# A streaming encoder layer on one core: the last two weight pairs in two sets of tokens, other forms of both norms, and weight preparation moved

## The chip, the core and the metric

The kernel runs on one core of a Trainium2 chip. The metric is the device time of one launch in microseconds: three runs of the kernel before gave 2345.38, 2347.2 and 2352.4, median 2347.2. The engines are named as in the profile: PE (TensorE, PEld its weight loads), DVE (VectorE), ACT (ScalarE), POOL (GpSimd), SP (SyncE, whose queue issues all DMAs here).

## The reference

One layer over 2048 prompt tokens and 64 sample tokens, width 1024, with a gated feed-forward part of width 2816. All inputs are float32.

```python
def trunk_layer(x, ...):
    mix, new_conv, new_ssm, new_k, new_v = token_mixers(x, ...)   # SSD scan and windowed attention, w_in, w_out
    h = layer_norm(DEEPNORM_ALPHA * x + mix, ln1_g, ln1_b)
    y = layer_norm(DEEPNORM_ALPHA * h + swiglu(h, w_gate, w_up, w_down), ln2_g, ln2_b)
    return y, new_conv, new_ssm, new_k, new_v

def swiglu(h, w_gate, w_up, w_down):
    g = jnp.einsum('bld,df->blf', h, w_gate)
    u = jnp.einsum('bld,df->blf', h, w_up)
    return jnp.einsum('blf,fd->bld', jax.nn.silu(g) * u, w_down)
```

## The kernel before

Every float32 operand of a matmul is scaled and split into two float16 parts (high, low); `mm3` multiplies with three matmuls (lines 112 to 114). The prompt is cut into eight blocks of 256 tokens (two tiles `t` of 128 rows each); the sample tokens are block 8 (`NB`).

Three stages follow each other. The first runs the input projection and the mixers block by block, and writes `mix` to DRAM. The second, `out_proj` (lines 879 to 888), goes through the blocks tile by tile: `op_rows` multiplies with `w_out` (two psum halves, added to the residual at line 821), takes `layer_norm` (lines 789 to 797: statistics by `bn_stats`, root by `rsqrt`, lines 98 to 108, a bit trick and three Newton steps of three instructions each) and normalises on DVE (line 825). One tile later `op_cols` transposes the tile, scales the columns on ACT (line 843), writes the residual for the second part after two POOL instructions (line 847), and once both tiles of a block are there forms seven operands of a Strassen-like scheme (POOL differences, lines 870 to 875), each split by `put` (ACT line 854, DVE line 855). For blocks 0 to 3, five of the seven operands go directly into the tiles `B0`; the rest goes to DRAM (`hd`). Blocks 0 and 1 (`EARLY`) run beside the last mixers.

The third stage is the feed-forward part. The 2816 columns are 11 pairs (`NP_`) of 2 x 128. The tokens are processed in two halves, h = 0 (blocks 0 to 3) and h = 1 (blocks 4 to 7 and the sample). In each half a pair p runs `gate`, then `flush` (the down products of the pair before), then `up`. `products` (lines 1053 to 1083) makes seven products of 512 token columns in four psum banks; three of them (2, 4 and 3) resume a bank whose first content ACT has copied before. `prep_w(p, m)` loads, scales, combines and splits the weights in h = 0 and writes them to DRAM (`ws`); h = 1 loads them from there. `prep_d` does so for the down weights. `scheme(h, p)` says whether the down product uses the scheme, too: only in h = 1 for p < 9. After the last pair of a half `last` takes the second norm of a block: statistics (`row_stats` on ACT or `bn_stats` on DVE), one `rsqrt` for the two rows of a block, normalisation on ACT (line 1282), multiply and add of the norm's parameters (lines 1284 and 1285) on DVE and POOL, with exceptions in `EG`, and the write of the output. In h = 1 the last pair (`LAST`) runs `up` ahead of `flush`, which then makes the down products of pairs 9 and 10 together.

The instructions of each engine run in the order that the scheduler of the tile framework gave them from the program order, a priority (`tc.high_priority` moves the statistics forward) and its estimate of durations. The memory pools matter at one point: `p2` and `apool` (norm tiles, `w_out`) are closed after the last `op_cols`, and `p3r`, which holds the temporaries `a`, the down weights and the last two operand tiles, is opened in their place. The pool `p3` (weights `w0`, `w1`, `raw`) is open from the third block on.

## Time and profile before

| | us |
|---|---|
| median of three runs | 2347.2 |
| the profiled execution | 2346.7 |
| its span, first to last instruction | 2344.8 |
| PE busy | 2167.7 (92%) |
| DVE busy | 1841.0 (79%) |
| ACT busy | 997.3 (43%) |
| POOL busy | 602.0 (26%) |
| mean granted clock of PE | 0.971 |

Busy time of an engine counts an instruction from its start to its end, waits inside an instruction included. Idle time of PE, 177 us in all, lies in the first 100 us, in the second stage (700 to 1000), around the change of halves (1660 to 1720) and after the last matmul.

### The profile page before, as it was taken

To read this page: it belongs to the slowest core of one execution; us is meant where nothing else is said; L and a number is where in the kernel's file an instruction comes from. 1 tells how busy PE (TensorE), PEld (TensorE's weight loads), DVE (VectorE), ACT (ScalarE), POOL (GpSimd) and SP (SyncE) were. 2 spreads that over 40 slices of the span, in tenths; PEclk is the share of its full clock that TensorE was granted. 3 is DMA by queue.
4 is the path that set the end of the run, shared out by engine and by line. 5 is a ranking of instruction groups with operands and counts; after the bars stand their busy time and mean duration, and the time that the engine had idled before them with its cause. 6 is when DMAs were issued, how large, how long until landed. Compare 5 with 4: busy or idle time off the path is not lost. (4 is left out here: it accounts for less than half of the span.)

```text
span 2344.8 us, 37764 instructions
## 1 busy us (share of the span) xinstructions
PE 2167.7 (92%) x14422; PEld 1267.5 (54%) x14422; DVE 1841.0 (79%) x4227; ACT 997.3 (43%) x1966; POOL 602.0 (26%) x462
## 2 busy tenths in 40 slices
PE   6899999999979798699999999999899999999993
PEld 5677777877865344244444444444445455555551
DVE  7786787788778999768777777775978777777768
ACT  6354454454464443465444544542333333333223
POOL 2111111111123466623222312311422222222404
PEclk9899999999989999799999999999999999999997
DMA  7000100100232544564333433446442222222202
GB/s 220 26 22 24 33 24 19 37 33 11 70 108 63 188 160 162 179 230 149 117 127 124 157 103 125 150 153 220 162 152 88 89 91 91 90 91 90 68 5 76
DMA packets 136025, 241.97 MB, mean 103 GB/s; under 512 B 20768, under 2 KB 53796, under 8 KB 135844
## 3 DMA queue, kind: packets, MB, share of 16 engines
q1 hardware_dynamic: 135844, 239.56, 30.5%
q8 instruction: 113, 1.85, 0.3%
q14 instruction: 68, 0.56, 0.1%
HBM read 155.61 MB, written 83.91 MB: 102 GB/s over the span
## 5 line engine op out<-in xcount | busy, mean ns | idle before, releaser
L112 PE MATMUL ps<-B,w 128*128 128x512 f16 x1232 | 469.6, 382 | 27.1 <-ACT w L950 16.0
L114 PE MATMUL ps<-B,w 128*128 128x512 f16 x1232 | 466.8, 382 | 4.7 <-DVE w L951 4.7
L113 PE MATMUL ps<-B,w 128*128 128x512 f16 x1232 | 470.2, 382 | 0.0
L112 PEld LDWEIGHTS <-w 128*128 128x128 f16 x2808 | 273.4, 99 | 179.3 <-ACT w L950 16.9
L113 PEld LDWEIGHTS <-w 128*128 128x128 f16 x2808 | 272.7, 99 | 177.6 <-issue 26.1
L114 PEld LDWEIGHTS <-w 128*128 128x128 f16 x2808 | 273.8, 99 | 174.3 <-issue 8.5
L112 PE MATMUL mm<-x,w 128*128 128x256 f16 (+1 forms) x1224 | 315.2, 268 | 7.4 <-ACT cin L426 3.0
L114 PE MATMUL mm<-x,w 128*128 128x256 f16 (+1 forms) x1224 | 315.2, 268 | 1.3 <-DVE w L240 1.3
L113 PE MATMUL mm<-x,w 128*128 128x256 f16 (+1 forms) x1224 | 315.1, 268 | 0.0
L1176 DVE SCALAR_TENSOR_TENSOR acc<-pds,ai,acc 128x512 f32<-128x512 f32 x208 | 152.5, 743 | 37.1 <-PE pds L114 36.9
L1176 DVE SCALAR_TENSOR_TENSOR acc<-pd,ai,acc 128x512 f32<-128x512 f32 x216 | 153.8, 741 | 27.1 <-PE pd L114 25.4
L951 DVE SCALAR_TENSOR_TENSOR w<-raw,fsc,w 128x512 f16<-128x512 f32 x176 | 148.3, 882 | 29.5 <-ACT w L950 29.5
L112 PE MATMUL pds<-wd,act 128*128 128x512 f16 x384 | 145.5, 379 | 3.3 <-DVE acc L1176 3.3
L113 PE MATMUL pds<-wd,act 128*128 128x512 f16 x384 | 145.5, 379 | 0.0
L114 PE MATMUL pds<-wd,act 128*128 128x512 f16 x384 | 145.4, 379 | 0.0
L987 ACT ACTIVATE wd<-rawd,fsc 128x512 f16<-128x512 f32 x120 | 80.6, 715 | 145.0 <-DVE fsc L91 76.4
L1074 POOL TENSOR_TENSOR a<-a 128x512 f32<-128x512 f32 x44 | 57.0, 1295 | 315.1 <-ACT a L1073 296.3
L950 ACT ACTIVATE w<-raw,fsc 128x512 f16<-128x512 f32 x176 | 114.0, 711 | 53.7 <-POOL raw L959 25.8
L1127 ACT ACTIVATE act<-a,asc 128x512 f16<-128x512 f32 x111 | 72.1, 711 | 125.3 <-DVE asc L91 122.8
L112 PE MATMUL pso<-wo,mt 128*128 128x512 f16 (+1 forms) x272 | 104.2, 385 | 16.3 <-DVE x L821 13.2
L847 POOL TENSOR_TENSOR x<-x,gb 128x1024 f32<-128x1024 f32 (+1 forms) x34 | 83.1, 2443 | 94.1 <-PE pth L839 81.7
L113 PEld LDWEIGHTS <-act 128*128 128x128 f16 x636 | 62.1, 98 | 82.8 <-issue 13.3
(398 smaller groups left out, 4492.9 us busy)
## 6 DMA issues: line engine op xcount, KB each, us to landing
ws<-w SPq DMA_DIRECT2D x176, 256.0 KB, 2.3
w<-ws SPq DMA_DIRECT2D x176, 256.0 KB, 2.9
rawd<-in_w_down SPq DMA_DIRECT2D x22, 1024.0 KB, 6.5
x<-in_x_prompt SPq DMA_DIRECT2D x32, 512.0 KB, 3.9
raw<-in_w_gate SPq DMA_DIRECT2D x11, 1024.0 KB, 5.5
raw<-in_w_up SPq DMA_DIRECT2D x11, 1024.0 KB, 7.5
hd<-ht SPq DMA_DIRECT2D x41, 256.0 KB, 2.0
B<-hd SPq DMA_DIRECT2D x41, 256.0 KB, 6.0
```

What stands on the lines that cost most here:

```text
L112: T.matmul(out, lh, rh, start=start, stop=False, **kw)
L113: T.matmul(out, lh, rl, start=False, stop=False, **kw)
L114: T.matmul(out, ll, rh, start=False, stop=stop, **kw)
L847: G.tensor_tensor(out=r, in0=r, in1=gb1[:L, j], op=ALU.mult if j == 0 else ALU.add)
L950: S.activation(w[i][:, 0], x, AF.Identity, scale=sc)
L951: V.scalar_tensor_tensor(out=w[i][:, 1], in0=x, scalar=sc, in1=w[i][:, 0], op0=ALU.mult, op1=ALU.subtract)
L987: S.activation(w[i][:, 0], x, AF.Identity, scale=sc)
L1074: G.tensor_tensor(out=s["7"], in0=s["7"], in1=s["5"], op=ALU.add)
L1127: S.activation(at[:, 0], x, AF.Identity, scale=asc)
L1176: V.scalar_tensor_tensor(out=acc[:, cs], in0=ps, scalar=ai, in1=acc[:, cs], op0=ALU.mult, op1=ALU.add)
```

## The change

- A new `rsqrt1` finds the root of one column: the addition of epsilon is part of its first instruction, and a Newton step has two instructions in place of three. `layer_norm` uses it and returns the factor and the offset; `op_rows` normalises with them on ACT instead of DVE.
- `prep_w(0, 0)` and `prep_w(0, 1)` come after the output projection of blocks 2 to 5, ahead of blocks 6, 7 and the sample, instead of after all of them. `prep_d(0, 0)` stays where it was.
- In h = 1 the pairs 9 and 10 run in two sets, first blocks 4 and 5 with the sample, then blocks 6 and 7: gate and up of both pairs for a set, its down products, with the second set's gate and up laid between. `products` takes 256 columns of the operand tiles then, and the gate and up weights of both pairs are loaded a second time (`load_ws`).
- `last` takes the root row by row; in h = 1 it doesn't use POOL or ACT for the normalisation, but two DVE instructions that subtract, scale and shift. Both rows of block 6 have their statistics on ACT, both rows of block 7 on DVE. In h = 0 ACT, DVE and POOL keep their parts.

```diff
+    def rsqrt1(v, eps, y, L=P):
+        w = small.tile([P, 1], F32, tag="rsw1", name="rsw1")[:L]
+        V.tensor_scalar(out=v, in0=v, scalar1=eps, scalar2=0.5, op0=ALU.add, op1=ALU.mult)
+        V.tensor_scalar(out=y.bitcast(I32), in0=v.bitcast(I32), scalar1=1, scalar2=None,
+                        op0=ALU.arith_shift_right)
+        V.tensor_scalar(out=y.bitcast(I32), in0=y.bitcast(I32), scalar1=-1, scalar2=0x5EF759DF - 2 ** 31,
+                        op0=ALU.mult, op1=ALU.add)
+        for _ in range(3):
+            V.scalar_tensor_tensor(out=w, in0=y, scalar=v, in1=y, op0=ALU.mult, op1=ALU.mult)
+            V.scalar_tensor_tensor(out=y, in0=w, scalar=-1.5, in1=y, op0=ALU.add, op1=ALU.mult)
...
-        V.tensor_scalar(out=ag[:L, 1:2], in0=ag[:L, 1:2], scalar1=eps_, scalar2=None, op0=ALU.add)
-        V.tensor_copy(mu_r[:L, 0:1], ag[:L, 0:1])
-        rsqrt(ag[:L, 1:2], mu_r[:L, 1:2], 1, L, "rsw2")
+        rsqrt1(ag[:L, 1:2], eps_, mr[:L, 0:1], L)
+        V.scalar_tensor_tensor(out=mr[:L, 1:2], in0=ag[:L, 0:1], scalar=-1.0, in1=mr[:L, 0:1],
+                               op0=ALU.mult, op1=ALU.mult)
...
-        V.tensor_scalar(out=r, in0=r, scalar1=mr[:L, 0:1], scalar2=mr[:L, 1:2],
-                        op0=ALU.subtract, op1=ALU.mult)
+        S.activation(r, r, AF.Identity, scale=mr[:L, 0:1], bias=mr[:L, 1:2])
...
-    todo = out_proj([b for b in range(NB + 1) if b not in EARLY], psp, "p", todo)
-    op_cols(*todo[:3], psm, "mm")
...
+    HEAD = 4
+    rest = [b for b in range(NB + 1) if b not in EARLY]
+    todo = out_proj(rest[:HEAD], psp, "p", todo)
+    prep0()
+    todo = out_proj(rest[HEAD:], psp, "p", todo)
+    op_cols(*todo[:3], psm, "mm")
...
+    def load_ws(p, m, order):
+        wts[p, m] = w_tiles(p, m, order)
+        for i in order:
+            Q.dma_start(out=wts[p, m][i], in_=wsd[p][m][i])
...
-                mm3(ps, w[i][:, 0, k], w[i][:, 1, k], B[i][:, :, 0, k], B[i][:, :, 1, k],
+                mm3(ps, w[i][:, 0, k], w[i][:, 1, k], B[i][:, g.qs, 0, k], B[i][:, g.qs, 1, k],
...
-                if end and j == 0 and b != 7:
+                if end and (b == 6 or j == 0 and b != 7):
...
-            rsqrt(v, rs, n, L)
+            for j in range(n):
+                rsqrt1(mv[:, j, 1:2], LN_EPS / ALPHA ** 2, rs[:, j:j + 1], L)
...
+            if end:
+                V.scalar_tensor_tensor(out=r, in0=r, scalar=mv[:, j, 0:1], in1=gb[2][:L, 0],
+                                       op0=ALU.subtract, op1=ALU.mult)
+                V.scalar_tensor_tensor(out=r, in0=r, scalar=rs[:, j:j + 1], in1=gb[2][:L, 1],
+                                       op0=ALU.mult, op1=ALU.add)
...
+    p, p1 = NP_ - 2, NP_ - 1
+    ga, gs, gb_ = Group(Bt, blocks(4, 6)), groups[1], Group(Bt, blocks(6, 8))
+    gate(p, [ga, gs])
+    flush(pend)
+    get_w(1, p1, 0)
+    get_w(1, p, 2)
+    up(1, p, [ga, gs])
+    get_w(1, p1, 1)
+    gate(p1, [ga, gs])
+    load_ws(p, 0, ORD)
+    get_w(1, p1, 2)
+    up(1, p1, [ga, gs])
+    load_ws(p, 1, ORD)
+    gate(p, [gb_])
+    norms2()
+    for g in (gs, ga):
+        for rows in g.rows:
+            prod(p, g, rows)
+            prod(p1, g, rows)
+    load_ws(p1, 0, ORD)
+    up(1, p, [gb_])
+    load_ws(p1, 1, ORD)
+    for g in (gs, ga):
+        for rows in g.rows:
+            last(rows, True)
+    gate(p1, [gb_])
+    up(1, p1, [gb_])
+    for rows in gb_.rows:
+        prod(p, gb_, rows)
+    for rows in gb_.rows:
+        prod(p1, gb_, rows)
+        last(rows, True)
```

## Rows read from the trace of the kernel before

**Rows 1.** The page: span, and busy us (share) xinstructions of each engine

```profile
span 2344.8 us, 37764 instructions
PE 2167.7 (92%) x14422; PEld 1267.5 (54%) x14422; DVE 1841.0 (79%) x4227; ACT 997.3 (43%) x1966; POOL 602.0 (26%) x462
```

**Rows 2.** Busy time by stretch: PE, PEld, DVE, ACT, POOL, granted clock, DMA share

```profile
876.01:902.00 25.99, 23.20 (x114) 11.17 (x113) 25.16 (x46) 10.05 (x25) 15.47 (x9) 1.00 0.58 192
...
960.00:980.00 20.00, 5.52 (x19) 2.32 (x20) 9.11 (x15) 4.07 (x12) 18.40 (x9) 0.59 0.48 170
980.00:1020.00 40.00, 36.18 (x149) 15.66 (x148) 23.30 (x39) 22.35 (x38) 9.02 (x7) 0.88 0.92 334
1640.00:1720.00 80.00, 67.58 (x422) 32.13 (x420) 78.32 (x152) 24.92 (x35) 32.89 (x16) 0.96 0.53 173
...
2280.00:2300.00 20.00, 20.00 (x139) 10.20 (x136) 18.06 (x60) 6.95 (x13) 0.00 (x0) 1.00 0.00 1
...
2305.50:2344.80 39.30, 0.03 (x1) 0.00 (x0) 32.71 (x55) 7.01 (x6) 20.93 (x8) 0.57 0.30 113
```

**Rows 3.** Timelines of DVE and POOL, second stage (start, us, engine, line, operation)

```profile
850.93 1.19 DVE L107 SCALAR_TENSOR_TENSOR rsw<-rsw,ag 128x1 f32<-128x1 f32 x1
...
876.89 1.19 DVE L107 SCALAR_TENSOR_TENSOR rsw<-rsw,ag 128x1 f32<-128x1 f32 x1
878.11 2.27 DVE L108 SCALAR_TENSOR_TENSOR mr<-rsw,mr 128x1 f32<-128x1 f32 x1
...
881.84 0.16 DVE L108 SCALAR_TENSOR_TENSOR mr<-rsw,mr 128x1 f32<-128x1 f32 x1
882.03 0.16 DVE L106 TENSOR_TENSOR rsw<-mr 128x1 f32<-128x1 f32 x1
...
886.90 5.44 DVE L855 TENSOR_TENSOR ht<-hs,ht 128x512 f16<-128x512 f32 x2
...
886.68 5.10 POOL L847 TENSOR_TENSOR x<-x,gb 128x1024 f32<-128x1024 f32 x2
```

**Rows 4.** Groups of instructions by shape: count, busy us, mean ns, idle before, releasers

```profile
L951 DVE SCALAR_TENSOR_TENSOR w<-raw,fsc,w 128x512 f16<-128x512 f32 x176 | 148.3, 882 | 29.5 <-ACT w L950 29.5
...
L825 DVE TENSOR_SCALAR x<-x,mr 128x1024 f32<-128x1024 f32 x16 | 15.6, 977 | 0.2
...
L1282 ACT ACTIVATE acc<-acc,nb,rs 128x1024 f32<-128x1024 f32 x16 | 18.9, 1231 | 52.8 <-DVE nb L1279 38.9 <-DVE rsw L107 13.9
```

**Rows 5.** Timelines of DVE, PE and ACT around the first gate

```profile
951.51 0.72 DVE L821 SCALAR_TENSOR_TENSOR x<-pso,iv,x 64x512 f32<-64x512 f32 x1
...
979.84 0.61 PE L112 MATMUL ps<-B,w 128*128 128x512 f16 x1 [13.64 <-ACT w L950]
...
988.00 0.60 ACT L1065 ACTIVATE a<-ps 128x512 f32<-128x512 f32 x1 [2.18 <-DMA hds<-ht]
```

**Rows 6.** PE's timeline, 256-column matmuls; then one 512-column piece of the chain

```profile
285.08 0.27 PE L114 MATMUL mm<-x,w 128*128 128x256 f16 x1
285.19 0.27 PE L112 MATMUL mm<-x,w 128*128 128x256 f16 x1
...
2291.50 0.22 PE pds L113
```

**Rows 7.** Timelines of DVE and POOL after the last matmul

```profile
2305.00 9.09 DVE L1277 TENSOR_SCALAR mv<-mv 128x2 f32<-128x2 f32 x1
...
2338.59 2.36 DVE L1285 TENSOR_TENSOR acc<-acc,gb 128x1024 f32<-128x1024 f32 x2
...
2304.85 4.63 POOL L1284 TENSOR_TENSOR acc<-acc,gb 128x1024 f32<-128x1024 f32 x2
```

**Rows 8.** DVE's timeline: five 512-column additions, one 128-column product; statistics by shape

```profile
1714.43 3.37 DVE L1176 SCALAR_TENSOR_TENSOR acc<-pd,ai,acc 128x512 f32<-128x512 f32 x5
...
2261.03 0.34 DVE L1108 SCALAR_TENSOR_TENSOR sgs<-pss,invs,sgs 128x128 f32<-128x128 f32 x1
...
L1274 DVE BATCH_NORM_STATS2 bs<-acc 128x6 f32<-128x512 f32 x26 | 17.7, 683 | 0.2
```

More of the change, by code (lines that the diff above doesn't have):

```diff
@@ L966, in prep_w, with prep0 @@
         wts[p, m] = w
+    def prep0():
+        for m in range(2):
+            prep_w(0, m)
+    HEAD = 4
[4 more added lines that the diff above has]
+    op_cols(*todo[:3], psm, "mm")
+    es_2.close()
+    es_w.close()
+    p3r = pool("p3r", ctx, bufs=1, side="right")
     def prep_d(h, p):
@@ L1019, in get_w @@
         else:
-            wts[p, m] = w_tiles(p, m, ORD + (0,))
-            for i in ORD + (0,):
-                Q.dma_start(out=wts[p, m][i], in_=wsd[p][m][i])
+            load_ws(p, m, ORD + (0,))
     sB = p3.tile([P, 2, 2, 4, DSEQ], F16, name="sB")
@@ L1051, in products_sample, with products @@
         return ps
-    def products(w, B):
-        s = {}
+    def products(w, g):
+        s, B = {}, g.B
+        tile4 = lambda x: x.rearrange("p (b c) -> p b c", b=4)[:, :g.nq]
         for i in ORD:
@@ L1094, in gate @@
                 continue
-            s = products(wts[p, 0], g.B)
+            s = products(wts[p, 0], g)
             g.sg = {}
@@ L1111, in up @@
             else:
-                s = products(wts[p, 1], g.B)
+                s = products(wts[p, 1], g)
                 for j, c in enumerate(CS):
@@ L1130, in put @@
             def put(i, x):
-                act[i] = (p3.tile([P, 2, 4, P], F16, tag="w0", bufs=10, name="actl") if (h, p) == LAST else
-                          p3r.tile([P, 2, 4, P], F16, tag="act", bufs=7, name="act"))
+                if g.nq == 4:
+                    act[i] = p3r.tile([P, 2, 4, P], F16, tag="act", bufs=7, name="act")
+                else:
+                    if i % 2:
+                        two[0] = p3r.tile([P, 2, 2, 2, P], F16, tag="act", bufs=7, name="act2")
+                    act[i] = two[0][:, (i - 1) % 2]
                 split(act[i], x)
+            two = [None]
             if g.sub:
@@ L1251, in row_stats @@
         junk = p3r.tile([P, 2, 512], F16, tag="wd", bufs=9, name="junk").rearrange("p l d -> p (l d)")[:L]
-        sm = small.tile([P, 2], F32, tag="sm", bufs=2, name="sm")
+        sm = small.tile([P, 2], F32, tag="sm", bufs=6, name="sm")
         S.activation(junk, r, AF.Identity, accum_out=sm[:L, 0:1])
@@ L1262, in last @@
         L = P if b < NB else DSEQ
-        mv = small.tile([P, 2, 2], F32, tag="mv", bufs=2, name="mv")[:L]
-        rs = small.tile([P, 2], F32, tag="mr", name="rs2")[:L, :n]
+        mv = small.tile([P, 2, 2], F32, tag="mv", bufs=6, name="mv")[:L]
+        rs = small.tile([P, 2], F32, tag="rs2", bufs=6, name="rs2")[:L, :n]
         nb = small.tile([P, 2], F32, tag="nb", name="nb")[:L, :n]
@@ L1288, in last, with prod, flush @@
                              O["y_s"].rearrange("b l d -> (b l) d")), in_=r)
-    LEAD = 1
     PRI = 400
-    EG = {(4, 0): (G, G), (4, 1): (G, G), (6, 1): (V, V), (7, 0): (G, V), (7, 1): (V, V)}
-    def flush(*pends):
-        if not pends[0]:
-            return
-        h, p, groups = pends[0]
-        end = pends[-1][1] == NP_ - 1
-        if end:
-            norms2()
-        steps = [(g, rows) for g in reversed(groups) for rows in g.rows]
-        def prod(q, g, rows):
-            if rows is g.rows[0]:
-                ai = g.acts[q][1]
-                V.tensor_tensor(out=ai, in0=ai, in1=invs[:, q, 2:3], op=ALU.mult)
-            if g.sub:
-                down_sample(q, g)
-                return
-            if q == 0:
-                for row in rows:
-                    acc_init(*row)
-            if scheme(h, q):
-                down(q, g, rows[0][0])
-                return
-            for row in rows:
-                down_rows(q, g, row, len(pends) == 2)
-        ahead = LEAD if len(pends) == 2 else 0
-        for i in range(len(steps) + ahead):
-            if i < len(steps):
-                prod(p, *steps[i])
-            if i >= ahead:
-                if len(pends) == 2:
-                    prod(pends[1][1], *steps[i - ahead])
-                if end:
-                    last(steps[i - ahead][1], h == 1)
-    for m in range(3):
-        get_w(0, 0, m)
+    def prod(q, g, rows):
+        if rows is g.rows[0]:
+            ai = g.acts[q][1]
+            V.tensor_tensor(out=ai, in0=ai, in1=invs[:, q, 2:3], op=ALU.mult)
+        if g.sub:
+            down_sample(q, g)
+            return
+        if q == 0:
+            for row in rows:
+                acc_init(*row)
+        if scheme(g.h, q):
+            down(q, g, rows[0][0])
+            return
+        for row in rows:
+            down_rows(q, g, row, g.nq < 4)
+    def flush(pend):
+        if not pend:
+            return
+        p, groups = pend
+        if p == NP_ - 1:
+            norms2()
+        for g in reversed(groups):
+            for rows in g.rows:
+                prod(p, g, rows)
+                if p == NP_ - 1:
+                    last(rows, False)
+    get_w(0, 0, 2)
     pend = None
+    blocks = lambda b0, b1: [[(b, 0), (b, 1)] for b in range(b0, b1)]
     for h in range(2):
```

60 lines of the change are left out of this document (25 added, 35 removed).

## The prediction, made before the change was run

> **What bounds the kernel now.** I read the page first: TensorE is busy for 92% of a span of 2344.8 us [rows 1], so some 177 us of idle TensorE is all that an edit of order can win; the work on TensorE itself stays the same. Next I read the busy time by stretch, to find where those 177 us lie. Three stretches matter here.
>
> First, the output projection with its norms (about 700 to 955). In a stretch of one block TensorE is busy for 23.2 of 26.0 us, VectorE for 25.2 [rows 2]. The timeline of VectorE shows the same block returning after 25.96 us, with no room in it [rows 3]. A good part of it isn't work: the tiny steps of the root (128x1) take 0.16 us when alone and 1.19 or 2.27 us while GpSimd runs, and two 512-column differences take 5.44 us beside a 5.10 us GpSimd pair [rows 3]. The trace thus shows VectorE instructions with two inputs in SBUF waiting until the GpSimd instruction ends. I count about 10 us of such waits in a block, 16 us of work.
>
> Second, the hole before the first gate: in 960 to 980 TensorE is busy for 5.5 of 20 us at a granted clock of 0.59 (between the levels of 1.2 and 2.4 GHz), and the next 40 us have 0.88 [rows 2]. The second product of pair 0 stops 13.64 us for ScalarE's weight instruction (L950), and the first copy of a product comes only at 988.00, released by the last write of the sample block [rows 5]. So the weights of pair 0 come late, and, apart from that, so does the memory that the old stage holds (p3r takes the place of p2 and apool).
>
> Third, the end: TensorE ends at about 2305.5, and 39.3 us follow with VectorE at 32.7 and GpSimd at 20.9 us [rows 2]. A 128x2 addition takes 9.09 us there, next to GpSimd's 4.63 us pairs [rows 7].
>
> Before that end, from 1720, TensorE is full (20.00 in 2280 to 2300 [rows 2]).
>
> **First norm.** Per tile of 128 rows VectorE loses the separate add, the copy, three of nine root steps and the 128x1024 normalisation, and gains one small product. In steps of 0.19 us for the dependent ones (881.84 to 882.03 [rows 3]) that is 3 x 0.19 + 0.07 + 0.1 - 0.19 = 0.55 us, plus the normalisation, at 0.98 us mean [rows 4], its 0.75 us step when unblocked: 1.3 us a tile, 2.6 a block. ScalarE gets 1.23 us instead [rows 4]; it has about 10 us busy in 26 [rows 2], so it hides there, and the tile is used one tile later, so its latency hides too. TensorE's own 23.2 us [rows 2] are the new floor, so a block falls from 25.96 to about 23.7: 2.2 us. From 803 to 950 there are 5.7 blocks: 12.5 us; the two blocks mixed with the last mixers before that I put at 4. Gain 16 (bounds 5, if the waits for GpSimd just shift, and 20).
>
> **Pair 0's weights amid the projections.** This moves two prep_w with all they issue: per matrix eight ScalarE puts, as many VectorE puts (0.88 mean), four GpSimd sums [rows 4], the absolute maxima, one maximum on TensorE, and the writes to ws on SP's queue, which now stand before the loads of the last blocks (their loads run one to two tiles early, so I put that at nothing; cover gone, it would be one landing, some 4 us). Unblocked, VectorE's part is 16 x 0.67 + 1.5 = 12 us, and GpSimd's 8 sums (half as wide as the pair of rows 3, so some 1.3 us each) bring waits: at the block's ratio (10 us of waits to 15 of GpSimd) 7 us. VectorE is full there, so the stage grows by 19 us (bounds 12 and, with every put blocked for a GpSimd pair as in rows 3, 32).
>
> What it buys: the sample block's second half is added at 951.51, and the first copy follows 36.5 us later [rows 5]. Without the preparation between them there stays the sample's own chain (root 2, normalisation 1.2, transposes 1, columns 3, splits and two writes) beside what GpSimd has left of block 7 and the sample, eight instructions of 1.3 to 2.5 us (14.5), and the last write (2): some 17 us. So 19.5 us return (bounds 14 and 25). What is late next is the memory of p3r and the load of the two last operand tiles, not the weights. After it, the down weights of pair 0 can be fetched earlier, since their buffer is free earlier, and the clock falls less: of 3.8 us idle and about 4 us of clock in 980 to 1020 [rows 2] I take 4 back.
>
> Front: 16 - 19 + 19.5 + 4 = 20.5 us gained, I take 20; bounds 0 and 42 (the hole closes wholly and TensorE bounds all).
>
> **Norms between the halves (h = 0).** They keep the ScalarE normalisation and GpSimd, but take the root row by row: 2 x 10 small instructions in place of 13 a block, 7 more, four blocks. VectorE is full there (78.3 of 80 in 1640 to 1720 [rows 2]). 28 x 0.1 to 0.19 us is 3 to 5 us, some hidden by TensorE's work. I take a loss of 3 (bounds -2 and +8).
>
> **Last two pairs in two sets.** Gate and up run on 256 columns, twice: 672 matmuls in place of 336. A 256-column matmul of the projections starts 0.11 us after the one before, with a load of its own each; one of 512 takes 0.22 [rows 6]. So TensorE's time stays within 1 us. Here a rule speaks against it: the Trainium skill, TensorE: Matmul & The Clock Gate, The mechanism, says that a weight load overlaps a running matmul only if their row groups differ; all of these loads use all rows. The 0.11 us spacing of rows 6 speaks against such a charge; I give it a rival below. The new loads of ws (28 of 256 KB) go on SP's queue behind buffers that the previous gate or up frees, 10 us or more ahead of use; the share of DMA in 2280 to 2300 is 0.00 [rows 2], so I put them at nothing; without cover one load is some 3 us.
>
> VectorE gets more. A 128-column instruction takes 0.34, one of 512 0.67 in a row of five [rows 8]; so 256 costs about 0.4 and a split pair 0.13 more: 40 pairs, 5 us. The norms' two products of 1024 move to it: nine more at 1.18 [rows 7], 10.6 us. From the gate of the second set to the last matmul TensorE has 9 + 25 + 27 + 21 = 82 us; VectorE's work from there to the end is (leftover up 7.5, gates 3, ups 14, adds of the down products 24 x 0.67 + 2.6, five norms of the first set 22, the last four rows 21) = 86 us. It fits, though with little slack.
>
> The new end: in the last 5.2 us of TensorE and after, VectorE has 4 additions (2.6), two rows with statistics on ScalarE (0.45 + 9 x 0.15 + 2 x 1.18 = 4.1 each) and two with its own (2 x 0.6 [rows 8] + 0.15 + 1.35 + 2.36 = 5.1 each): 21 us, so it ends about 16.5 us after TensorE with a us of chain, and the last write takes what it takes now, 3.9 us (2344.8 less 2340.95 [rows 1, 7]). 20.4 in place of 39.3: 19 us gained if VectorE has no backlog. For waits of TensorE in the half-width sets and some backlog I take off 5: 14 (bounds 3 and 20).
>
> **Sum.** The profiled run took 2346.7 us, its span 2344.8 and 1.9 around it; the median of the three runs is 2347.2, so the sum stands half a us below what I compare with. 2346.7 - 20 + 3 - 14 = 2315.7, say 2316.
>
> **Rivals.**
> A: the front gives nothing. The weights' preparation lengthens the full VectorE stretch by the 32 us of its upper bound, which cancels the hole's 19.5 + 4 and half of the first norm's gain. For it: VectorE's waits [rows 3]. Against: ScalarE's share relieves it. 2346.7 + 3 - 14 = 2336.
> B: the end gains little. VectorE's 86 us run 11 us behind, so that the last rows' norms queue behind the first set's. For: 86 of 98 us available. Against: no GpSimd lock there any more. 2346.7 - 20 + 3 - 3 = 2327.
> C, slower: TensorE waits for ScalarE within the half products. Products 2, 4 and 3 resume a bank that ScalarE must have copied, and the cover falls from one product of 12 x 0.22 = 2.6 us to 1.3. There are 8 such calls, 24 points. A copy takes about 0.4 us, so it costs only if something stands before it, a row statistic for instance. At 1.2 us each it is 29 us, which leaves the kernel as it was; from 1.6 us each (38 us) it is slower, about 2355. Against: ScalarE is busy for 7 of 20 us in 2280 to 2300 [rows 2].
> D, slower too: the weight load isn't covered at half width. 336 more loads, each taken as long as the half matmul that follows it (0.11), are 37 us: 2353. That the projections keep a spacing of 0.11 with a load for each [rows 6] speaks against. The skill's rule above would give this one.
> E: the hole closes and TensorE bounds the whole front (42), the end gives 17: 2346.7 - 42 - 17 = 2288, with the half norms at nothing. For: TensorE needs just 23.2 us a block. Against: the memory of p3r still comes after the sample's chain. If the change doesn't do what it says, because the preparation is still put behind the last blocks on the engines' queues, the front is 12.5 + 4: 2346.7 - 16 + 3 - 14 = 2320, inside the forecast's range.
>
> **Chances.** Forecast 0.62 (that last case within it), A 0.14, B 0.10, E 0.08, C 0.04, D 0.02. A measurement of this kernel can tell about 0.3%, 7 us, from no change: faster is below 2340. Faster: 0.60 of the forecast, 0.10 of A, 0.10 of B and 0.08 of E: 0.88. Within: 0.02 of the forecast and 0.04 of A: 0.06; slower: C and D, 0.06. The range: forecast's sum with half of each bound gives 2300 to 2334; it must reach A's 2336 and towards E's 2288: 2293 to 2337 leaves about 0.2 out (most of E, C and D, and the forecast's and A's far ends).
>
> **What would show it.** In the profile after: L951 of pair 0 before the last blocks' additions; TensorE's idle 955 to 980 cut to under 10 us; a block period under 24.5 us; the normalisation of x on ScalarE with 1.2 us; GpSimd idle after the last pair; TensorE full in the half sets at a spacing of 0.11; about 20 to 24 us from its last matmul to the end. It would be wrong if VectorE's full stretch grows by more than 25 us, if the hole stays, or if TensorE shows idle time between the half products.

## The result, and the profile after

| | before | changed |
|---|---|---|
| timed, us: median (range, runs) | 2349.8 (2345.4 to 2353.0, 4) | 2320.7 (2320.1 to 2322.4, 4) |
| ratio, 95% interval | | 0.9875 (0.9856 to 0.9895) |
| profiled execution, span, us | 2344.8 | 2320.6 |

2316 was predicted, with 2293 to 2337 around it: the time lies in the range, 4.7 us above the forecast. The spans of the two profiled executions are only 24.2 us apart, the medians 29.1. Of the 4.9 us between these two figures 3.6 lie ahead of the change: the first addition of the output projection (VectorE, block 0) starts here, before, then changed.

```profile
712.52 0.75 DVE L821 SCALAR_TENSOR_TENSOR x<-pso,iv,x 128x512 f32<-128x512 f32 x1 [0.39 <-PE pso L114]
716.09 0.75 DVE L833 SCALAR_TENSOR_TENSOR x<-pso,iv,x 128x512 f32<-128x512 f32 x1 [0.52 <-PE pso L126]
```

Up to this addition every kernel of this document runs 1829 VectorE instructions, and no edit touches one of them; still its start varies from 710.4 to 716.1 us between the profiled executions. Counted from it, kernels with the same front reach the first copy of a product within 0.2 us of each other (266.3 to 266.5 in four of them). So where times of two executions are compared, they are counted from the first addition. The span counted so is 1632.3 us before and 1604.5 changed: 27.8 us apart, near the 29.1 of the medians.

The page of the changed kernel, against [rows 1]: span and busy us of each engine.

```profile
span 2320.6 us, 38579 instructions
PE 2172.3 (94%) x14762; PEld 1302.8 (56%) x14762; DVE 1834.2 (79%) x4264; ACT 1015.0 (44%) x2006; POOL 579.5 (25%) x457
```

TensorE's work has hardly changed (2172 for 2168 us); the gain is idle time. Busy time by stretch in the changed kernel, against [rows 2]; columns as there: PE, PEld, DVE, ACT, POOL, granted clock, DMA share, GB/s.

```profile
850.00:902.00 52.00, 49.04 (x245) 24.20 (x244) 50.86 (x87) 28.42 (x55) 36.28 (x20) 1.00 0.57 194
902.00:928.00 26.00, 19.37 (x82) 8.49 (x81) 24.53 (x29) 12.60 (x25) 21.35 (x13) 0.87 0.64 220
...
960.00:980.00 20.00, 16.02 (x76) 7.91 (x75) 18.12 (x23) 11.63 (x28) 15.89 (x8) 0.93 0.41 154
980.00:1020.00 40.00, 36.81 (x165) 16.73 (x165) 22.55 (x46) 21.25 (x36) 8.36 (x6) 0.92 0.80 284
...
1640.00:1720.00 80.00, 68.72 (x416) 32.17 (x414) 79.25 (x167) 27.87 (x41) 30.34 (x16) 0.94 0.52 179
...
2280.00:2300.00 20.00, 19.56 (x99) 9.38 (x98) 15.34 (x34) 3.40 (x7) 0.00 (x0) 1.00 0.00 0
2301.40:2320.60 19.20, 0.04 (x1) 0.00 (x0) 15.05 (x54) 1.58 (x4) 0.00 (x0) 0.57 0.28 109
```

Three things stand here. The hole of 960 to 980 is mostly filled (16.0 for 5.5 us of TensorE), but a new dent has come at 902 to 928, where the first pair's weights are now prepared: TensorE 19.4 of 26 us at a granted clock of 0.87 (between the levels of 1.2 and 2.4 GHz). And behind the last matmul 19.2 us are left where there were 39.3, without GpSimd.

Timelines of the changed kernel around the first gate, first VectorE, then TensorE, then ScalarE, against [rows 5] (start, us, engine, line, operation, idle before and its releaser).

```profile
964.60 0.73 DVE L833 SCALAR_TENSOR_TENSOR x<-pso,iv,x 64x512 f32<-64x512 f32 x1
...
983.19 0.59 PE L124 MATMUL ps<-B,w 128*128 128x512 f16 x1 [6.70 <-ACT a L1082]
...
970.93 1.24 ACT L837 ACTIVATE x<-x,mr 64x1024 f32<-64x1024 f32 x1 [4.46 <-DVE mr L809]
...
982.54 0.60 ACT L1082 ACTIVATE a<-ps 128x512 f32<-128x512 f32 x1 [1.68 <-DMA hds<-ht]
```

L833 is the second-half addition of the sample (L821 before), L1082 the first copy of a product (L1065 before). From the one to the other it is 17.9 us, where it was 36.5; but the addition comes 13.1 us later (964.60 for 951.51), 9.5 counted from the first addition. So the hole closed as forecast, and the first copy is only 9.0 us earlier (266.5 for 275.5, counted).

### The profile page after: what moved, and what is told of

It reads as the page before. It is cut to its first block, busy times and chain, and to the rows that moved or that the text cites. A ratio compares the mean times of both kernels' runs of the same rounds, so it can differ in the third digit from the quotient of the medians.

```text
span 2320.6 us, 38579 instructions
## 1 busy us (share of the span) xinstructions
PE 2172.3 (94%) x14762; PEld 1302.8 (56%) x14762; DVE 1834.2 (79%) x4264; ACT 1015.0 (44%) x2006; POOL 579.5 (25%) x457
## 5 line engine op out<-in xcount | busy, mean ns | idle before, releaser
L124 PE MATMUL ps<-B,w 128*128 128x512 f16 (+1 forms) x1344 | 486.0, 363 | 10.3 <-ACT a L1082 6.7
L125 PE MATMUL ps<-B,w 128*128 128x512 f16 (+1 forms) x1344 | 487.0, 363 | 0.0
L126 PE MATMUL ps<-B,w 128*128 128x512 f16 (+1 forms) x1344 | 484.0, 362 | 0.0
L125 PEld LDWEIGHTS <-w 128*128 128x128 f16 x2920 | 283.8, 99 | 167.3 <-issue 24.5
L126 PEld LDWEIGHTS <-w 128*128 128x128 f16 x2920 | 285.0, 99 | 156.7 <-issue 7.1
L124 PEld LDWEIGHTS <-w 128*128 128x128 f16 x2920 | 284.9, 99 | 153.3 <-issue 6.7
L956 DVE SCALAR_TENSOR_TENSOR w<-raw,fsc,w 128x512 f16<-128x512 f32 x176 | 151.3, 898 | 33.1 <-ACT w L955 33.1
L1199 DVE SCALAR_TENSOR_TENSOR acc<-pd,ai,acc 128x512 f32<-128x512 f32 x216 | 153.2, 742 | 21.6 <-PE pd L126 20.1
L124 PE MATMUL pds<-wd,act 128*128 128x512 f16 x416 | 158.1, 380 | 7.9 <-DVE acc L1199 7.4
L125 PE MATMUL pds<-wd,act 128*128 128x512 f16 x416 | 158.2, 380 | 0.0
L126 PE MATMUL pds<-wd,act 128*128 128x512 f16 x416 | 157.3, 380 | 0.0
L1091 POOL TENSOR_TENSOR a<-a 128x512 f32<-128x512 f32 (+1 forms) x48 | 59.0, 1228 | 365.9 <-ACT a L1090 326.6
L1144 ACT ACTIVATE act<-a,asc 128x512 f16<-128x512 f32 (+1 forms) x123 | 76.4, 683 | 128.2 <-DVE asc L91 125.5
L125 PEld LDWEIGHTS <-act 128*128 128x128 f16 x668 | 65.6, 98 | 86.3 <-issue 14.0
L126 PEld LDWEIGHTS <-act 128*128 128x128 f16 x668 | 65.2, 98 | 81.6 <-DVE act L1145 3.5
## 6 DMA issues: line engine op xcount, KB each, us to landing
w<-ws SPq DMA_DIRECT2D x204, 256.0 KB, 3.0
ws<-w SPq DMA_DIRECT2D x176, 256.0 KB, 2.1
hd<-ht SPq DMA_DIRECT2D x41, 256.0 KB, 2.0
B<-hd SPq DMA_DIRECT2D x41, 256.0 KB, 5.4
```

What stands on the lines that cost most here:

```text
L124: T.matmul(out, lh, rh, start=start, stop=False, **kw)
L125: T.matmul(out, lh, rl, start=False, stop=False, **kw)
L126: T.matmul(out, ll, rh, start=False, stop=stop, **kw)
L956: V.scalar_tensor_tensor(out=w[i][:, 1], in0=x, scalar=sc, in1=w[i][:, 0], op0=ALU.mult, op1=ALU.subtract)
L1091: G.tensor_tensor(out=s["7"], in0=s["7"], in1=s["5"], op=ALU.add)
L1144: S.activation(at[:, 0], x, AF.Identity, scale=asc)
```

## The experiments

Two tables carry the argument. A marker is an instruction that both kernels have: the sample's second-half addition, the first copy, and an up-projection of the second half (the first product of a pair with its gate, L1132 in the changed kernel, at 2037.5 before). In the second half the up-projections follow one another every 59.2 us in all kernels, so the last marker is the cleanest; in the first half the up-projection can stand before or behind a few products of the pair before. All times in us; those of the first table count from the first addition, whose own start stands in the third column. Counted so, the kernel before has 239.0, 275.5, 1325.0 and 1632.3.

**The front, with the new end in all four:**

| kernel | timed median | first addition | sample's addition | first copy | marker | end of span |
|---|---|---|---|---|---|---|
| neither edit at the front | 2333.8 | 713.3 | 238.9 | 275.3 | 1323.8 | 1616.7 |
| first norm alone | 2322.5 | 714.1 | 226.6 | 260.8 | 1314.2 | 1607.1 |
| moved preparation alone | 2338.4 | 715.7 | 256.0 | 276.4 | 1327.5 | 1620.4 |
| both (the changed kernel) | 2320.7 | 716.1 | 248.5 | 266.5 | 1311.3 | 1604.5 |

**The end, with the new front in all four:**

| kernel | timed median | marker (start in the span) | last matmul ends | marker to there | from there to the end |
|---|---|---|---|---|---|
| old order, old norms | 2335.2 | 2025.7 | 2293.8 | 268.0 | 39.6 |
| old order, new finish | 2327.1 | 2026.7 | 2294.8 | 268.0 | 29.9 |
| two sets, old finish | 2332.7 | 2025.9 | 2308.0 | 282.1 | 21.5 |
| two sets, new finish (changed) | 2320.7 | 2027.4 | 2301.4 | 274.1 | 19.2 |

"Finish" is what follows the root: normalisation, product and sum. The second and third rows both have the short root, which the first hasn't, so it is counted with either edit.

**The preparation put back.** The rest is the changed kernel.

```diff
-    todo = out_proj(rest[:HEAD], psp, "p", todo)
-    prep0()
-    todo = out_proj(rest[HEAD:], psp, "p", todo)
+    todo = out_proj(rest, psp, "p", todo)
...
+    prep0()
     get_w(0, 0, 2)
```

> The changed kernel, with the first pair's preparation put back behind all blocks; the short root, the ACT normalisation and the new end stay. Theory from the forecast (the move costs 19 us among the projections, returns 19.5 us of the hole and 4 us of clock): this kernel is 4.5 us slower than the changed one, some 2325 us. Rival from the changed kernel's trace (the sample's second-half addition came 13.1 us later although the norms had gained about 9.6, so the move costs 22.7; the hole shrank from 36.5 to 17.9, so it returns 18.6): the move is worth nothing, this kernel lies within 4 us of the changed one on the other side, 2317 to 2321 us. In its trace the sample's second-half addition should stand near 942 us and the first copy of a product some 36 us later, near 978.

2322.5 us (2321.7 to 2323.7), 1.8 above the changed kernel: between the two theories, and too little to tell from nothing. The addition stands at 940.7 and the first copy at 975.0, as expected. So with the new norm, counted from the first addition, the move costs 21.9 us of the projections (226.6 to 248.5) and takes 16.3 out of the hole (34.2 to 17.9). Another 8.8 us come back between the first copy and the up-projection at 1585.4 (869.3 counted, for 872.5 without the move). In all the move gains 2.9 us at the marker. Part of the 8.8 is visible as TensorE's idle time from 1100 to 1580, 7.3 us without and 3.8 with the move; the rest isn't traced to an instruction.

**The old first norm.**

```diff
-        rsqrt1(ag[:L, 1:2], eps_, mr[:L, 0:1], L)
-        V.scalar_tensor_tensor(out=mr[:L, 1:2], in0=ag[:L, 0:1], scalar=-1.0, in1=mr[:L, 0:1], ...)
+        V.tensor_scalar(out=ag[:L, 1:2], in0=ag[:L, 1:2], scalar1=eps_, scalar2=None, op0=ALU.add)
+        V.tensor_copy(mr[:L, 0:1], ag[:L, 0:1])
+        rsqrt(ag[:L, 1:2], mr[:L, 1:2], 1, L, "rsw2")
...
-        S.activation(r, r, AF.Identity, scale=mr[:L, 0:1], bias=mr[:L, 1:2])
+        V.tensor_scalar(out=r, in0=r, scalar1=mr[:L, 0:1], scalar2=mr[:L, 1:2],
+                        op0=ALU.subtract, op1=ALU.mult)
```

> The changed kernel with the first norm as before (the root of three instructions per step, the normalisation on VectorE); the moved preparation and the new end stay. Theory from the forecast (a block's period falls from 25.96 to 23.7 us, 16 us in the stage): 16 us slower than the changed kernel, some 2337 us. Rival from the trace of the changed kernel (a lead of only 3.4 us at the fourth-last block, then 2.1 us for each block): about 10 us slower, 2330 us. If it is under 5 us slower, PE or POOL, not VectorE, set the period of the blocks.

2338.4 us, 17.7 slower than the changed kernel. That looks like the 16 of the forecast, but the first table says otherwise: without the move the norm is worth 11.3 (2333.8 to 2322.5), with it 17.7. The two edits aren't independent. With the old norm the move loses 4.6 us, with the new one it gains 1.8; at the marker, counted, it loses 3.7 and gains 2.9. The table shows where they part. Among the projections the move costs 17.0 us on the old norm and 21.9 on the new one, and the hole returns 16.0 and 16.3. Behind the first copy the new norm gets 8.5 us back and the old one loses 2.7 more. Why the first pairs differ so isn't shown.

**The front alone, and the end alone.** The first is the kernel before with both edits of the front, the second the changed kernel with both of them taken back (the two diffs above together).

> The kernel before with the two edits at the front alone (first norm, first pair's preparation among the projections); its end and all its last norms are as before. Theory from the forecast: 20 us faster than the kernel before. Rival from the trace of the changed kernel (its up-projections of the second half lead those of before by 10.1 us at 1919 and at 2037 us): about 10 us faster, 13 if the new norms between the halves cost the 3 us that were forecast.

> The kernel before with the end alone: last two pairs in two sets of tokens and last norms without GpSimd (those between the halves too); its front is as before. Theory from the forecast: 14 us from the end less 3 us between the halves, 11 us faster than the kernel before. Rival from the two traces (24.2 us of span gained, 10.1 of them ahead of the last pairs): 14 us faster, with the last matmul some 19 us ahead of the span's end where it was 39.3. If front and end don't meet anywhere, this gain and that of the front alone add up to that of both.

Front alone: 2335.2, 14.2 faster than before (2349.3, ratio 0.993 to 0.9955): less than the theory's 20, just above the rival's 10 to 13. End alone: 2333.8, 15.5 faster (0.9923 to 0.9947), with 18.9 us behind the last matmul: the rival's 14 and 19, not the theory's 11. Together 29.7, and both at once gave 29.1: the two ends of the kernel don't meet. In the traces, counted from the first addition, the front is worth 13.7 to 13.9 us at the marker (1325.0 before, 1311.3 and 1311.1 with the new front) and the end 14.1 behind it (307.3 to 293.2).

**The end's two parts.** First two sets with the norms finished as before (the short root and the changed statistics stay); then the order of before with the new finish.

```diff
...
-            if end:
-                V.scalar_tensor_tensor(out=r, in0=r, scalar=mv[:, j, 0:1], in1=gb[2][:L, 0], ...)
-                V.scalar_tensor_tensor(out=r, in0=r, scalar=rs[:, j:j + 1], in1=gb[2][:L, 1], ...)
-            else:
-                ...
+            S.activation(r, r, AF.Identity, scale=rs[:, j:j + 1], bias=nb[:, j:j + 1])
+            e1_, e2_ = EG.get((b, j), (V, G)) if end else (V, G)
+            e1_.tensor_tensor(out=r, in0=r, in1=gb[2][:L, 0], op=ALU.mult)
+            e2_.tensor_tensor(out=r, in0=r, in1=gb[2][:L, 1], op=ALU.add)
...
```

> The changed kernel with the last norms finished as before: normalised on ScalarE, then product and sum with gain and bias on VectorE and GpSimd as the kernel before deals them out; the two sets, the short root and the front stay. Theory 1 (the sets do it: half of the last norms lie beside products, whoever does them): within 4 us of the changed kernel, 2321 to 2325 us. Theory 2 (GpSimd's 5.1 us sums and their hold on VectorE do it): 6 to 10 us slower than the changed kernel, 2327 to 2331 us, and the span behind the last matmul is 25 to 29 us in place of 19.

2332.7 us: 12 slower than the changed kernel, so the sets alone are worth 2.4 (2335.2 to 2332.7), less than the 7 us over which this kernel's runs lie. My second theory had the sign, was short in size (6 to 10 us) and named the wrong place. The tail is short, 21.5 us; the loss lies ahead of the last matmul, where TensorE needs 282.1 us from the marker instead of 274.1. Busy time of that kernel by stretch, then the timelines of its VectorE and its GpSimd in the same place, and two of TensorE's waits in 2240 to 2300 (what for: us in total, times, longest).

```profile
2240.00:2260.00 20.00, 20.00 (x137) 13.23 (x136) 19.41 (x61) 8.20 (x13) 9.58 (x5) 1.00 0.24 67
2260.00:2280.00 20.00, 14.06 (x113) 11.32 (x111) 18.08 (x39) 7.28 (x14) 8.42 (x5) 0.91 0.26 105
```

```profile
2256.36 3.41 DVE L119 SCALAR_TENSOR_TENSOR rsw<-rs,mv 128x1 f32<-128x1 f32 x2
2259.69 2.38 DVE L120 SCALAR_TENSOR_TENSOR rs<-rsw,rs 128x1 f32<-128x1 f32 x2
...
2252.77 4.67 POOL L1308 TENSOR_TENSOR acc<-acc,gb 128x1024 f32<-128x1024 f32 x2 [1.44 <-ACT acc L1306]
2257.39 4.66 POOL L1309 TENSOR_TENSOR acc<-acc,gb 128x1024 f32<-128x1024 f32 x2
```

```profile
PE ps L124 <- DVE a L1097: 2.7, 1, 2.7
PE ps L124 <- DVE a L1094: 1.6, 1, 1.6
```

The first set's norms stand beside the second set's products. While GpSimd works at them, two root steps of VectorE take 3.41 us and the next two 2.38, where four of the same take 0.60 us behind the last matmul of the changed kernel. The products' sums (L1094, L1097) queue behind them on VectorE, TensorE waits for these, and it falls to 14.06 of 20 us. Of the 18.1 us that the sets take out of the tail (39.6 to 21.5), 14.1 come back ahead of it: 6.1 with either finish (268.0 to 274.1), 8.0 more with GpSimd's. This edit puts the normalisation back on ScalarE, too; no run parts that from GpSimd's share.

> The changed kernel with the old order of the end: the last two pairs over all four blocks, their products row by row, and only the finish of the norms is new (two instructions per row on VectorE, nothing on ScalarE's normalisation or GpSimd). Theory 1 (the sets do it): all eight rows' finish lies on VectorE behind the last pair's products, so 10 us or more slower than the changed kernel, 2331 us or more, the span behind the last matmul stays above 30 us. Theory 2 (GpSimd does it): within 5 us of the changed kernel.

2327.1 us: neither theory. The new finish alone takes 8.1 us (2335.2 to 2327.1), and the tail shows it (39.6 to 29.9), since TensorE's part doesn't change (268.0). By the timed medians the sets give 2.4, the finish 8.1 and both 14.4. By the traces, from the marker to the end, they give 4.1, 9.7 and 14.5. So it stays open whether a part of the gain comes only with both.

**What GpSimd costs VectorE among the projections.** The product and the sum of the first norm's rows with gain and bias are left out for the residual, so this kernel computes something else and serves as a measurement alone.

```diff
-        for j in range(2):
-            G.tensor_tensor(out=r, in0=r, in1=gb1[:L, j], op=ALU.mult if j == 0 else ALU.add)
```

> The changed kernel without the product and the sum with gain and bias that GpSimd makes of each row set of the first norm for the residual (left out altogether, so the residual is the bare norm). It takes some 10 us of GpSimd from each row set and nothing from VectorE. Theory (GpSimd's instructions hold VectorE's small ones): the period of a block falls from 23.9 us by 2 us or more, the sample's second-half addition comes at 955 us or before. Rival (VectorE's own work sets the period): it stays within 0.5 us of 23.9 and the addition within 3 us of 964.6.

2296.5 us (two runs), 24.2 less. Nothing was taken from VectorE, yet it is less busy. Busy time by stretch, of about one block each: first the new norm without the move, then the kernel without gain and bias.

```profile
867.70:891.50 23.80, 22.61 (x113) 11.14 (x112) 23.04 (x38) 12.48 (x25) 15.50 (x8) 1.00 0.65 209
```

```profile
800.00:822.40 22.40, 22.40 (x114) 11.16 (x112) 17.14 (x41) 13.10 (x28) 5.40 (x4) 1.00 0.65 213
```

Some six us of a block's VectorE time (23.04 for 17.14) are waits for these two GpSimd instructions. The block falls from 23.85 us (867.7 to 891.5 and its neighbours) to 22.4 and TensorE becomes the bound, full at 22.40 of 22.40; so the period falls by 1.45 us and not by the theory's 2, while the addition comes far ahead of its 955. The sample's addition, at 927.7, is 33.2 us earlier than in the changed kernel (counted from the first addition, 215.3 for 248.5), and 11.4 of these are won by the addition that stands at 796.1 here and at 811.2 there: up to it the norms of the first blocks share VectorE with the last mixers. Not all of the lead lasts: at the third up-projection it is 24.4 us, at the marker 23.1. In the changed kernel, VectorE and then GpSimd:

```profile
759.32 6.07 DVE L576 SCALAR_TENSOR_TENSOR y<-xT,dcol,y 128x128 f32<-128x128 f32 x4
...
759.01 2.35 POOL L858 TENSOR_TENSOR x<-x,gb 128x1024 f32<-128x1024 f32 x1 [5.72 <-PE pth L850]
761.31 1.32 POOL L881 TENSOR_TENSOR hs<-hs,hs 128x512 f32<-128x512 f32 x1
762.59 2.39 POOL L858 TENSOR_TENSOR x<-x,gb 128x1024 f32<-128x1024 f32 x1
```

Four products of 128x128 take 6.07 us, just as long as three GpSimd instructions in a row. One by one, three of the four end 0.14 to 0.15 us behind a GpSimd instruction each (at 761.50, 762.77 and 765.13, for 761.35, 762.63 and 764.98), and the fourth, with none beside it, takes 0.34. The Trainium skill says why (SBUF — State Buffer, SBUF: two separate sides): VectorE with two inputs in SBUF and GpSimd share one pair of ports, which whoever comes first holds for its whole instruction. The trace agrees with that.

**Half of the preparation moved.** Only the gate's weights are prepared among the projections.

```diff
...
-    prep0()
+    prep_w(0, 0)
+    raw1 = load_raw(0, 1)
     todo = out_proj(rest[HEAD:], psp, "p", todo)
...
+    prep_w(0, 1, raw1)
     get_w(0, 0, 2)
```

> The changed kernel with only half of the moved preparation among the projections: the first pair's gate weights stay behind the fourth block of the rest, its up weights (their load stays there) are prepared behind the last block, while the gate's products run. Theory: the move costs what it takes of a full VectorE (23.9 us at the sample's second-half addition with the new norm: 940.7 without it, 964.6 with it) and the hole needs the gate weights alone; so the addition comes at about 953 and the hole stays near 18 us, the kernel is 8 to 12 us faster than the changed one, some 2310 us. Rival: VectorE and ScalarE are as full between 960 and 1010 (18.1 of 20 us for VectorE in 960:980), the up weights come late, PE waits some 10 us for them near 1000 and the time is within 2 us of the changed kernel.

2320.0 us (2318.2 to 2323.9): no difference shown. The span of its profiled execution is 4.2 us shorter, but as much stands ahead of the first addition already (711.8 for 716.1). Counted from there the sample's addition comes 2.8 us earlier (245.7), and at the marker nothing is left (1311.4 for 1311.3). The theory's 8 to 12 us fall: half the preparation costs the stage 19.1 of the 21.9 us.

**Towards a faster kernel: gain and bias later.** If GpSimd's two instructions cost 24 us, VectorE might do their work among the pairs, where it is busy for 75.4 of 100 us (1100 to 1200 in the changed kernel). The sample alone keeps GpSimd's two instructions; the rest is done behind the first pair's up-projection, in each half.

```diff
+        if b == NB:
             for j in range(2):
                 G.tensor_tensor(out=r, in0=r, in1=gb1[:L, j], op=ALU.mult if j == 0 else ALU.add)
...
+            if p == 0:
+                gain_bias([row for rows in groups[0].rows for row in rows])
```

> The changed kernel with the first norm's gain and bias moved out of the projections: the residual rows of the eight blocks go to memory bare, and after the first pair's up-projection of each half VectorE multiplies and adds them in the accumulators (four instructions of 128x512 a row, about 0.69 us each, 22 us a half); the sample's row stays as it was. Theory (what GpSimd holds VectorE back among the projections is worth the 24 us that the kernel without gain and bias is faster, and VectorE has some 6 us idle in 30 among the pairs): 24 us less the part of 44 us that finds no idle VectorE, up to 10 us a half: 2300 to 2312 us. Rival (the pairs lose what the projections gain, since VectorE's 22 us stand ahead of the first flush and PE waits for its banks): within 4 us of the changed kernel or slower.

2322.7 us: the rival. Counted from the first addition (714.8 for 716.1), the sample's addition is 33.2 us ahead of the changed kernel. At the second up-projection (1049.9 for 1069.6) 18.4 are left, at 1635.2 (for 1652.5) 16.0, and at 1735.4 (for 1731.3) none: minus 5.4. The two losses, 15 and 21 us, stand where VectorE has the 22 us of each half. But the first isn't the price of these 22 us alone: the kernel without gain and bias, which puts nothing in that place, loses 8.8 us of its lead by the third up-projection, too. Against that kernel this one is 7.0 us behind at 1635.2, ahead of the second half's 22 us, and 28.5 at 1735.4, so the first 22 us cost some 7 and the second 21. Busy time of that kernel in these two places, then what TensorE waited for in 900 to 1060 (us in total, times, longest):

```profile
980.00:1020.00 40.00, 24.44 (x102) 10.30 (x103) 33.76 (x63) 14.25 (x24) 13.85 (x9) 0.79 0.36 126
...
1640.00:1700.00 60.00, 38.70 (x252) 19.14 (x251) 59.83 (x132) 20.52 (x30) 20.86 (x10) 0.84 0.54 175
```

```profile
PE ps L124 <- ACT w L956: 13.6, 2, 12.9
```

VectorE takes the additions ahead of the small steps that make pair 1's scale, ScalarE's weights (L956 there) wait 10.4 us for the scale and TensorE for the weights; between the halves VectorE was full before it got 22 us more.

> As the run before, but the sums with the bias stand on GpSimd (16 of 128x512 a half, 1.3 us each) and the products alone on VectorE (11 us a half). Theory (VectorE's time is what is short): 2 to 5 us faster than with both on VectorE. Rival (GpSimd's hold on VectorE costs as much there as among the projections): the same time or slower than with both on VectorE.

2332.6 us, 10 slower than with both on VectorE, though VectorE has 11 us a half less to do: GpSimd holds it among the pairs as well. Counted from the first addition (710.4), this kernel is 19.9 us behind the one with both on VectorE at 1582.1, and 10.8 at the marker. How the loss spreads over the pairs I haven't followed.

> The run with gain and bias on VectorE later, and of the first pair's weights the gate's alone prepared among the projections, the up weights behind the last block. Theory (the earlier run with the gate's weights alone brought the addition of the sample 7.1 us forward and its up-projections of the second half 4.2 us; with less GpSimd work the stage has more room, so half of that is left): within 3 us of the run with gain and bias later and both weights moved, on the fast side. Rival (with the holds gone the whole preparation fits among the projections): 3 us or more slower than that run.

2321.9 us, 0.9 below the run with both weights moved: the theory's side, but no difference shown. Of the 7.1 us that the theory starts from, some 4 lay ahead of the first addition, as said above.

The last run moves gain and bias of the first half's blocks alone, and behind the scale of pair 1's up weights; blocks 4 to 7 and the sample keep GpSimd's.

```diff
+        if b >= 4:
...
+                    V.scalar_tensor_tensor(out=a, in0=a, scalar=one, in1=gbq[i], op0=ALU.mult, ...)
...
+                one = small.tile([P, 1], F32, name="one")
+                V.tensor_scalar(out=one, in0=invs[:, 1, 1:2], scalar1=0.0, scalar2=1.0, ...)
```

> The changed kernel with gain and bias of the first norm moved for the blocks 0 to 3 alone (the first half's rows): VectorE multiplies and adds them behind the scale of pair 1's up weights (the instructions read a one that is worked out from it), ahead of the first flush; blocks 4 to 7 and the sample keep GpSimd's product and sum among the projections. Theory (the run with all rows later lost 15 us where its 22 us of VectorE stood ahead of pair 1's gate weights, and 21 where the other 22 us stood in the full stretch between the halves; the lead of the early blocks was 12.6 us at 799): the lead at the sample's second-half addition is about 15 us, the first pairs cost 5 of it, nothing is lost between the halves, so 2308 to 2314 us, faster than the changed kernel and the kernel before. Rival (VectorE's 22 us stand in the way in any place ahead of the first flush): within 4 us of the changed kernel.

2325.6 us, 4.8 slower than the changed kernel: the theory falls, and the loss is a little more than the rival's 4. Counted from the first addition (714.2), the lead is 12.4 us at the sample's addition and 13.0 at 1054.7; at the next up-projection (1124.0) it is gone (the kernel without gain and bias loses 8.5 us in the same place), and at 1538.0 it is minus 6.1. Of that kernel, by stretch:

```profile
1020.00:1060.00 40.00, 31.80 (x123) 13.09 (x124) 39.04 (x58) 12.49 (x20) 13.64 (x8) 0.83 0.29 99
1060.00:1100.00 40.00, 37.99 (x178) 17.60 (x177) 33.79 (x65) 21.95 (x36) 9.98 (x7) 1.00 0.41 145
1100.00:1160.00 60.00, 57.23 (x267) 26.25 (x265) 45.23 (x82) 27.16 (x46) 16.63 (x12) 1.00 0.38 132
```

Here the 22 us fill VectorE (39.04 of 40) one pair later, and TensorE is idle for 13.0 us in these three stretches, where the changed kernel has 3.8. No kernel that computes the whole layer was found that beats the changed one by more than the runs differ.

## Why the prediction was right, point by point

The gain came out at 29.1 us for the 31 of the sum, but not term by term: the front gives some 6 us less than forecast, the norms between the halves don't take the 3 that were subtracted for them, and the end gives what was said. That the gain is only 2 us short is in part luck, since two of the misses cancel by half. The rest of the 4.7 us is the start of the sum: it goes from 2346.7, and the median of before came out at 2349.8.

**First norm: the mechanism right, 12 us for 16.** The block's period fell to 23.85 us, 23.7 forecast. From about 809 to the sample's addition this gave 11.1 us for the 12.5 of the forecast (counted from the first addition, 96.2 and 95.0 at 809, then 238.9 and 226.6). The mis-sized term is "the two blocks mixed with the last mixers before that I put at 4": 1.2 us. What holds VectorE up there is mostly not the work that the edit removes: leaving out GpSimd's gain and bias wins 11.4 us in the same place. The reason given for 23.7 was wrong as well: "TensorE's own 23.2 us are the new floor". Without gain and bias a block takes 22.4, so TensorE's floor is lower, and with the new norm VectorE, at 23.04 of 23.80, still sets the period.

**Preparation amid the projections: each figure near, the sum not.** 19 us were forecast with bounds of 12 and 32; it was 17.0 on the old norm and 21.9 on the new one. The hole's new length, 17 forecast, is 17.9; its old one is 34.2 with the new norm alone, so 16.3 return and not 19.5. Clock and idle time behind it, 4 forecast, gave 8.8. The sum is plus 3.2 us at 1585 and 2.9 at the marker, for the plus 4.5 of the forecast. I treated the two edits of the front as two terms to be added. They aren't: on the old norm the move loses 3.7 us at the marker, and the difference arises behind the first copy (8.5 us returned on the new norm, 2.7 lost on the old one), where I had one figure of 4 for both.

**The front as a whole** is worth 13.7 us at the marker (14.2 by the timed runs of the front alone), where 20 were forecast, and that is the miss, of which the norms between the halves (next) gave 3 back. 3.7 are from the norm (16 to 12.3) and 1.6 from the move (4.5 to 2.9). The remaining 1.0 is the balance of shifts behind the sample's addition that weren't followed: there the lead of the norm alone shrinks from 12.3 to 9.6 us. Rival A, that the front gives nothing, falls. The 32 us that it takes for the preparation were 17.0 and 21.9, and by its own terms (16 - 32 + 23.5) it should have left 7.5 us of gain and not none.

**Norms between the halves: nothing instead of a loss of 3.** From the eleventh up-projection of the first half (1598.1 before, 1585.4 changed) to the second of the second half (1742.4 and 1731.3) it takes 144.3 us before and 143.9 with the new root, on the old front; 145.6 and 145.9 on the new one. VectorE is just as full as it was (79.25 of 80 for the 78.32 of [rows 2]).

**The end: 14 forecast, 14.1 found, and both parts hold.** From 39.3 us behind the last matmul 19.2 are left, so 20.1 were won where I had 19; TensorE takes 274.1 us from the marker to its end where it took 268.0, a loss of 6 where I had taken 5 off. Idle time between the half products was one of my signs of being wrong, and some of it is there. TensorE's waits in 2040 to 2310 (what for: us in total, times, longest):

```profile
PE pd L124 <- DVE acc L1199: 1.3, 2, 0.8
PE pdt L125 <- DVE acts L1145: 0.7, 1, 0.7
PE pmx L78 <- DVE ama L96: 0.6, 1, 0.6
PE pds L124 <- ACT act L1144: 0.4, 1, 0.4
```

These are 3.0 us. Read from the start of one matmul to the start of the next, ten matmuls come late by 4.8 us in all, these waits included; in the kernel before there are two such places, with 0.2 us. Of the rest 0.8 us are the 336 further matmuls and 0.4 four more small ones for the maximum. No wait for a product's copy is among the waits, so rival C falls. Rival D falls by the spacing of the half-width products in the changed kernel, each with a load of its own, at the 0.11 us of [rows 6]:

```profile
2200.13 0.27 PE L125 MATMUL ps<-B,w 128*128 128x256 f16 x1
2200.24 0.27 PE L126 MATMUL ps<-B,w 128*128 128x256 f16 x1
2200.35 0.27 PE L124 MATMUL ps<-B,w 128*128 128x256 f16 x1
2200.46 0.27 PE L125 MATMUL ps<-B,w 128*128 128x256 f16 x1
```

So the rule by which a load overlaps only with other row groups (the Trainium skill, TensorE: Matmul & The Clock Gate, The mechanism) doesn't hold for these loads. Rival B falls too: VectorE has 15.34 of 20 us before the end, no backlog. Rival E fell since the hole kept its 17.9 us, and TensorE never bounded the projections.

The tail itself came out nearly as worked out. VectorE's last instructions in the changed kernel, against [rows 7], with four root steps between them:

```profile
2302.95 1.27 DVE L1307 SCALAR_TENSOR_TENSOR acc<-acc,mv,gb 128x1024 f32<-128x1024 f32 x1
...
2309.39 0.60 DVE L119 SCALAR_TENSOR_TENSOR rsw<-rs,mv 128x1 f32<-128x1 f32 x4
...
2312.78 3.67 DVE L1309 SCALAR_TENSOR_TENSOR acc<-acc,rs,gb 128x1024 f32<-128x1024 f32 x3
```

VectorE ends at 2316.45, 15.0 us behind TensorE (16.5 forecast), and the span 4.2 us later (3.9 forecast). What I hadn't worked out is what each of the end's two edits gives alone: 2.4 and 8.1 us by the timed runs, 4.1 and 9.7 by the traces.

## What to carry to other kernels

Price an instruction that is put on GpSimd by the VectorE instructions that it holds, and price work moved beside other work by who is held there: here 12 of the 14.4 us that the new end gives were gone with GpSimd finishing the norms beside the products. When two edits change the same stage, work out the second on the profile that the first one leaves; here their terms didn't add. An engine that is idle a quarter of the time is not free for more: 22 us put on VectorE among the pairs cost some 7 in one place and 21 in another, where what stood behind them was awaited. And before times of two profiled executions are compared, look where they stand ahead of the first changed instruction: here they differed by up to 5.7 us there, more than some of the edits are worth.

## What the runs showed of the hardware that I had not expected

- Taking 34 GpSimd instructions out (L858, 2.45 us in the median) took 24.2 us off the kernel, though GpSimd is busy for only 15.50 of the 23.80 us of a block with the new norm; VectorE's busy time in a block fell by 6 us with no instruction of its own removed. A busy VectorE in this profile is partly a waiting one.
- TensorE's busy time of 23.2 us in a block [rows 2] isn't its floor: the same projections ran in 22.4.
